# Gated DeltaNet: another order around the triangular inverse (wider squares of k and q, a new table of weight splits, z's last chunk earlier)

## The chip, the cores and the metric

The kernel runs on one core of a Trainium2 chip. Its time is the device time of that core in microseconds (us). Five engines work in parallel, each in its own fixed order: TensorE (PE in the profile; PEld is its weight load), VectorE (DVE), ScalarE (ACT), GpSimd (POOL) and SyncE (SP), which issues most transfers. An instruction that waits holds up everything behind it on its engine.

## The reference

A trunk of two layers over 256 tokens of width 1024. Each layer is half a SwiGLU, a token mixer, half a SwiGLU; the mixer of layer 0 is a gated DeltaNet with 8 heads of 128, that of layer 1 windowed attention. Only the first mixer is touched:

```python
proj = h @ w_in                       # q, k, v (1024 columns each), z (1024), b, a (8 each)
qkv = silu(causal_depthwise_conv(qkv, w_conv))          # 4 taps along time
q = l2norm(q) * 128 ** -0.5; k = l2norm(k)              # x / sqrt(sum x*x + EPS)
beta = sigmoid(b); g = -exp(A_log) * softplus(a + dt_bias)
# per head and chunk of time, g summed up along the chunk:
L   = strict_lower((k * beta) @ k.T * decay)
sol = solve((I + L), [v * beta, k * beta * exp(g)])     # unit triangular
u, w = sol
# then over the chunks: v_new = u - w S;  o = (q exp(g)) S + (q k.T * decay) v_new
#                       S = S exp(g_last) + (k exp(g_last - g)).T v_new
y = (rmsnorm(o, out_norm) * silu(z)) @ w_out
```

All is float32. A product with a weight is made of three fast products: the weight is split in a high half (`whi`) and the rest (`wlo`), and so are the activations.

## The kernel before, in words

A chunk of 256 columns of `w_in` (`wcols`) comes as two pieces of 512 KB (`raw`, four buffers). `split` casts each to `whi` on ACT (L307) and makes `wlo = raw - whi`, on DVE as one instruction (L309) or on GpSimd as four (L314); `npool` says for how many of the chunk's two pieces GpSimd does it. `whi` and `wlo` have five buffers each. The products are L360 to L362: a chunk has two halves of 24 products each (8 rows of blocks by three products, and each piece serves four of these rows).

`gdn` runs through the chunks in the order z 0 and 1, z 2, k 0 to 3, v 0 to 3, q 0 to 2, z 3, q 3. `conv` does a chunk of k, v or q: 24 products into a PSUM tile `pcv` (four such buffers), the first tap on ACT into `cv` and three taps on DVE (L924), silu on ACT. Behind a chunk, generators go on by a step at each `tick` of a ticker, so that their work mixes into the products of the next chunks:

- `kpost`: transposes a chunk of k (`pkn`), copies it twice to `kk2` (`kd` and `keg` are its halves; L726, L727), sums the squares (`sumsq`, four squares with accumulators on ACT, L718), multiplies k by itself (`pkk`), makes `br` and `nbr` on DVE (L739 to L742) and scales `kd` and `keg` on GpSimd (L744, L745).
- `blocks(g)`, after k 1 and k 3, for half the heads: cuts out the 32x32 diagonal blocks (`d32`, L762), scales them (L765) and masks them (`tri16` and `off16`, L767), all on GpSimd, and makes a power for v's scale (`ks`, L769).
- `inverse`, after k 3: inverts all 16x16 diagonal blocks on DVE (L777 to L815, 22 instructions that depend on each other), in three steps with a yield between, and adds the two generators `chain(0)` and `chain(1)`, which double the blocks to 128x128 by small products (`pt1`, `py`, `px`) with copies between.
- `vpost` and `qpost`: transposition, scale, squares and products of v and q. `state` and `first` do the recurrence; `post` and `turn` normalise the output (`so`, `fo`, `on`) and transpose it (`poT`).

The order on each engine is set when the program is compiled: a scheduler with a model of the engines' times takes the instructions that are ready, in program order where it can choose. `issue_after(ins)` ties an instruction behind another. `self.hold = [a, b, ins...]` lets a weight pieces pass and ties the casts and splits of the next ones, until b pieces are through, behind `ins`.

Of the kernel before, what the change touches and what calls it, by code (L numbers as in the profile page):

```python
# [11 lines left out]
AF = mybir.ActivationFunctionType  # L12
# [201 lines left out]
class Kern:  # L214
# [162 lines left out]
    def proj_T(self, out, w, f, nrm):  # L377
        fs = slice(f * P, (f + 1) * P)
        for k in range(KT):
            wh, wl = w(k, fs)  # L380
            self.mm3(out, wh, wl, nrm.h.hi(k), nrm.h.lo(k), k == 0, k == KT - 1)
# [296 lines left out]
    def gdn(self, nrm, prep, w_in, w_out, after):  # L678
# [43 lines left out]
        def kpost(c):  # L722
            g, hs = c // 2, slice(2 * c, 2 * c + 2)
            loc = slice(2 * (c % 2), 2 * (c % 2) + 2)
            pv = transp(lambda i: kT[:, 2 * c + i, :], "pkn")
            nc.scalar.copy(kd[:, hs, :], pv[:, 0])  # L726
            nc.scalar.copy(keg[:, hs, :], pv[:, 1])  # L727
            sumsq(pv, ssk, 2 * c)
            yield
            beta, eG, eS = res["beta"], res["eG"], res["eS"]  # L730
# [7 lines left out]
            a = ssk[:, :, hs]  # L738
            nc.vector.tensor_scalar_add(a, a, EPS)  # L739
            nc.vector.reciprocal(br[:, :, hs], a)  # L740
            nc.vector.tensor_mul(br[:, :, hs], br[:, :, hs], beta[:, :, hs])
            nc.vector.tensor_scalar_mul(nbr[:, :, hs], br[:, :, hs], -1.0)  # L742
# [10 lines left out]
        def blocks(g):  # L753
# [4 lines left out]
            us = slice(8 * g, 8 * g + 8)  # L758
            raw = self.y1([P, 8, 32], "d32")
# [6 lines left out]
            for j, m in enumerate(("tri16", "off16")):  # L766
                nc.gpsimd.tensor_tensor(out=d2[:, j, us, :], in0=raw,  # L767
                                        in1=M[m].unsqueeze(1).to_broadcast([P, 8, 32]), op=ALU.mult)
            nc.gpsimd.tensor_tensor(out=sv[:, :, gs], in0=ssk[:, :, gs],  # L769
                                    in1=self.phalf.rearrange("p (t h) -> p t h", t=NT), op=ALU.pow)  # L770

        def inverse():
# [21 lines left out]
            yield  # L794
# [13 lines left out]
            yield  # L808
# [6 lines left out]
            nc.vector.transpose(yx[:, 1].rearrange("p u c -> p (u c)"), yx[:, 0].rearrange("p u c -> p (u c)"))  # L815
            late["yx"] = yx
            tk.add(chain(0), chain(1))

        def chain(g):
# [14 lines left out]
            nc.scalar.copy(t32, blockwise(self.psB("pt1"), off, X0))  # L834
# [79 lines left out]
        def conv(col0, dst, npool, start):  # L914
            w = self.wcols(w_in, col0, npool)
            for f in range(2):
                ct = col0 // P + f
                ps = self.psA("pcv")
                self.proj_T(ps[:, :T], w, f, nrm)
                c = self.c1([P, T], "cv")  # L920
                nc.scalar.activation(c, ps[:, :T], AF.Copy, scale=wc[:, 3, ct:ct + 1])
                for j in (2, 1, 0):
                    s = 3 - j
                    nc.vector.scalar_tensor_tensor(  # L924
                        out=c[:, s:], in0=ps[:, 0:T - s], scalar=wc[:, j, ct:ct + 1],
                        in1=c[:, s:], op0=ALU.mult, op1=ALU.add)
# [11 lines left out]
        def zgate(t, hs, keep=lambda ins: ins):  # L938
            z = zs[:, t, hs]
            keep(nc.scalar.activation(z, z, AF.Silu))  # L940
            keep(nc.gpsimd.tensor_tensor(
                out=z, in0=z, in1=onb.unsqueeze(1).to_broadcast([P, hs.stop - hs.start, P]), op=ALU.mult))
# [7 lines left out]
        def then(*steps):  # L950
            for st in steps:
                r = st()
                if r is not None:
                    yield from r
                    yield
# [11 lines left out]
        def zmore(n):  # L967
            for c in range(zc[0], zc[0] + n):
                w = self.wcols(w_in, 3 * D + c * 256)
# [6 lines left out]
        for c in range(4):  # L976
# [5 lines left out]
            conv(D + c * 256, lambda f: kT[:, 2 * c + f, :], c // 2, [then(*steps)])  # L982
# [96 lines left out]
        for c in range(4):  # L1079
# [292 lines left out]
```

## Time and profile before

| what | value |
|---|---|
| median of three runs | 1023.0 us (1020.8, 1023.0, 1023.43) |
| the profiled execution | 1021.12 us |
| its span | 1019.3 us |
| its granted TensorE clock, mean | 0.995 |
| PE busy | 999.8 us, 98% |
| DVE, ACT, POOL busy | 641.8, 551.7, 242.6 us |
| the DeltaNet stage | about 195 to 372 us of the span |
| DVE in 272 to 298 us | 25.97 of 26.00 us busy |

The times of the trace count from the start of the span. A line of the trace's timeline has start, duration, engine, line, operation, output and inputs with their tile names, shapes and, in brackets, the idle time ahead of it and what ended it. A row of a grouped view has the count, the busy time, the mean of one in ns and the idle time ahead. Lines (L777 and so on) are those of the kernel before.

### The profile page before, as it was taken

To read this page: it belongs to the slowest core of one execution; us is meant where nothing else is said; L and a number is where in the kernel's file an instruction comes from. 1 tells how busy PE (TensorE), PEld (TensorE's weight loads), DVE (VectorE), ACT (ScalarE), POOL (GpSimd) and SP (SyncE) were. 2 spreads that over 40 slices of the span, in tenths; PEclk is the share of its full clock that TensorE was granted. 3 is DMA by queue.
4 is the path that set the end of the run, shared out by engine and by line. 5 is a ranking of instruction groups with operands and counts; after the bars stand their busy time and mean duration, and the time that the engine had idled before them with its cause. 6 is when DMAs were issued, how large, how long until landed. Compare 5 with 4: busy or idle time off the path is not lost.

```text
span 1019.3 us, 16506 instructions
## 1 busy us (share of the span) xinstructions
PE 999.8 (98%) x6195; PEld 871.7 (86%) x6195; DVE 641.8 (63%) x971; ACT 551.7 (54%) x1007; POOL 242.6 (24%) x311
## 2 busy tenths in 40 slices
PE   8999999999989899999999999999999999999997
PEld 7888888899979788888888888888898678888886
DVE  5866654666894666666646666664578756666544
ACT  5756544457856545555434555553367646555432
POOL 0125510017852201222200123220021402222100
PEclk9999999999999999999999999999999999999999
DMA  7766666644452336666666666676563426666661
GB/s 247 236 187 194 198 198 178 202 138 149 128 168 64 104 104 203 187 189 192 198 191 186 188 185 200 186 199 200 188 200 111 144 89 212 197 186 186 204 188 42
DMA packets 135317, 177.05 MB, mean 174 GB/s; under 512 B 7251, under 2 KB 120261, under 8 KB 135237
## 3 DMA queue, kind: packets, MB, share of 16 engines
q1 hardware_dynamic: 132032, 171.46, 55.2%
q10 hardware_dynamic: 3204, 4.53, 1.6%
q8 instruction: 49, 0.80, 0.3%
q14 instruction: 32, 0.25, 0.1%
HBM read 174.92 MB, written 1.05 MB: 173 GB/s over the span
## 4 chain that ended last, share of the span: by engine, by line
PE 63%; issue 1%; DVE 1%; DMA 1%; ACT 0%; SPq 0%; POOLq 0%; POOL 0%; ACTq 0%
PE pg L367 11%; PE pu L367 11%; PE acc L362 7%; PE acc L360 7%; PE acc L361 7%; PE pu L368 6%; PE pg L368 6%; PE pgu L362 1%; PE pgu L361 1%; PE pgu L360 1%; PE pq L360 1%; PE pq L362 1%; PE pq L361 1%; PE psc L1196 1%; PE po L1240 1%
## 5 line engine op out<-in xcount | busy, mean ns | idle before, releaser
L309 DVE TENSOR_TENSOR wlo<-raw,whi 128x1024 fp32r<-128x1024 f32 (+1 forms) x304 | 375.1, 1237 | 201.3 <-ACT whi L307 199.9
L307 ACT CAST whi<-raw 128x1024 fp32r<-128x1024 f32 (+1 forms) x318 | 330.3, 1046 | 184.1 <-PE acc L362 82.6
L367 PE MATMUL pg<-hs,whi 128*128 128x512 f32 x624 | 218.7, 392 | 0.0
L367 PE MATMUL pu<-hs,whi 128*128 128x512 f32 x624 | 218.4, 391 | 0.0
L368 PE MATMUL pu<-hs,wlo 128*128 128x256 f32 x624 | 175.1, 281 | 0.0
L368 PE MATMUL pg<-hs,wlo 128*128 128x256 f32 x624 | 174.3, 280 | 0.0
L475 POOL TENSOR_TENSOR act<-act,gate 128x256 f32<-128x256 f32 x78 | 58.5, 750 | 353.2 <-DVE act L474 338.6
L367 PEld LDWEIGHTS pg<-hs,whi 128*128 128x128 f32 x624 | 116.7, 187 | 25.7
L367 PEld LDWEIGHTS pu<-hs,whi 128*128 128x128 f32 x624 | 116.7, 187 | 25.5
L361 PE MATMUL acc<-wlo,ah 128*128 128x512 f32 (+1 forms) x340 | 128.4, 378 | 0.0
L362 PE MATMUL acc<-whi,al 128*128 128x512 f32 (+1 forms) x340 | 128.3, 377 | 0.0
L360 PE MATMUL acc<-whi,ah 128*128 128x512 f32 (+1 forms) x340 | 127.8, 378 | 0.0
L368 PEld LDWEIGHTS pg<-hs,wlo 128*128 128x128 f32 x624 | 117.9, 189 | 0.4
L368 PEld LDWEIGHTS pu<-hs,wlo 128*128 128x128 f32 x624 | 117.9, 189 | 0.0
L360 PEld LDWEIGHTS acc<-whi,ah 128*128 128x128 f32 x340 | 64.0, 188 | 12.0
L361 PEld LDWEIGHTS acc<-wlo,ah 128*128 128x128 f32 x340 | 64.0, 188 | 11.8
L362 PEld LDWEIGHTS acc<-whi,al 128*128 128x128 f32 x340 | 63.9, 188 | 11.9
L478 POOL TENSOR_SCALAR ah<-act 128x256 fp32r<-128x256 f32 x78 | 66.4, 852 | 6.7
L464 ACT COPY gate<-pg 128x256 f32<-128x256 f32 x78 | 28.8, 369 | 55.3 <-PE pg L368 55.3
L473 ACT COPY act<-pu 128x256 f32<-128x256 f32 x78 | 28.9, 370 | 53.8 <-PE pu L368 53.8
L360 PE MATMUL pcv<-hs,whi 128*128 128x256 f32 x192 | 55.1, 287 | 2.3 <-DVE cv L924 2.3
L99 POOL TENSOR_TENSOR rst<-var,mhalf 128x1 f32<-128x1 f32 x10 | 5.6, 557 | 213.8 <-DVE var L97 213.8
(340 smaller groups left out, 1584.4 us busy)
## 6 DMA issues: line engine op xcount, KB each, us to landing
raw<-in_ffn_w_gu_dram SPq DMA_DIRECT2D x156, 512.0 KB, 4.3
raw<-in_ffn_w_down_dram SPq DMA_DIRECT2D x88, 512.0 KB, 4.2
raw<-in_a_w_in_dram SPq DMA_DIRECT2D x32, 512.0 KB, 4.2
raw<-in_ffn_w_gu_dram SPq DMA_DIRECT2D x40, 256.0 KB, 4.7
raw<-in_b_w_in_dram SPq DMA_DIRECT2D x12, 512.0 KB, 4.8
raw<-in_a_w_out_dram SPq DMA_DIRECT2D x8, 512.0 KB, 3.7
raw<-in_b_w_out_dram SPq DMA_DIRECT2D x8, 512.0 KB, 3.6
nw<-in_ffn_norm_dram ACTq DMA_DIRECT2D x3, 512.0 KB, 4.1
```

The source lines that it names most:

```text
L307: nc.scalar.copy(hi[:, c], raw[:, c])
L309: nc.vector.tensor_tensor(out=lo[:, c], in0=raw[:, c], in1=hi[:, c].bitcast(F32), op=ALU.subtract)
L360: nc.tensor.matmul(out, lhsT=lh, rhs=rh, start=start, stop=False)
L361: nc.tensor.matmul(out, lhsT=lh, rhs=rl, start=False, stop=False)
L362: return nc.tensor.matmul(out, lhsT=ll, rhs=rh, start=False, stop=stop)
L367: nc.tensor.matmul(out, lhsT=lh, rhs=r2, start=start, stop=False)
L368: return nc.tensor.matmul(out[:, :T], lhsT=ll, rhs=rh, start=False, stop=stop)
L464: nc.scalar.copy(g, pg[:, T:])
L473: nc.scalar.copy(a, pu[:, T:])
L475: nc.gpsimd.tensor_tensor(out=a, in0=a, in1=gates[f], op=ALU.mult)
L478: ahead[2] = nc.gpsimd.tensor_scalar(oh, a, 1.0, None, op0=ALU.mult)
L1196: nc.tensor.matmul(out, lhsT=qT[:, j, b * P:(b + 1) * P], rhs=kz[:, kv, :, kt * P:(kt + 1) * P], start=True, stop=True)
```

## The change

- The squares of a chunk of k or q are one instruction of 512 columns on ACT, written in place in PSUM, and a sum on DVE, in place of four squares with accumulators. The two copies to `kk2` become one. `br` and `nbr` move from `kpost` to `blocks`, for four heads at once.
- The scaling of `kd` and `keg` moves to a generator `kscale`, tied on GpSimd behind the last mask (`late["d"]`); the power `ks` is tied there as well.
- `inverse` has no yields and no longer adds the chain. The three taps on DVE of v's second chunk are tied behind its end (`late["inv"]`), and so is the split of the second piece of v's third chunk.
- `chain`, `kscale`: added after v's second chunk; the chain's first products are tied behind the last products of a `conv` called so far (`late["mm"]`).
- `npool` may name the pieces. k 0 to 3: 0, 0, 1, 1 of two pieces on GpSimd becomes 0, 1, 1, 0; v 0 to 3: the second piece each becomes none, both, the first, the second; z 3: none becomes the second.
- z's chunk 3 moves from behind q's chunk 2 to behind v's chunk 0. z's gate is multiplied on GpSimd in pieces of two heads.

```diff
     def wcols(self, w, c0, npool=0):
         src = w[:, c0:c0 + 256].rearrange("(k p) f -> p k f", p=P)
+        pool = npool if isinstance(npool, tuple) else range(2 - npool, 2)
         pieces = [self.wpiece(src[:, 4 * i:4 * i + 4, :], 4, 256,
-                              eng=self.nc.gpsimd if i >= 2 - npool else None) for i in range(2)]
+                              eng=self.nc.gpsimd if i in pool else None) for i in range(2)]
...
         def sumsq(pv, ss, h0):
-            for i in range(2):
-                for t in range(NT):
-                    j = self.small([P, P], "junk", 1)
-                    nc.scalar.activation(j, pv[:, t, i, :], AF.Square, accum_out=ss[:, t, h0 + i:h0 + i + 1])
+            nc.scalar.activation(pv, pv, AF.Square)
+            nc.vector.tensor_reduce(out=ss[:, :, h0:h0 + 2], in_=pv, axis=AX.X, op=ALU.add)
...
-            nc.scalar.copy(kd[:, hs, :], pv[:, 0])
-            nc.scalar.copy(keg[:, hs, :], pv[:, 1])
+            nc.scalar.copy(kk2[:, :, hs, :], pv)
...
-            yield
-            nc.gpsimd.tensor_tensor(out=kd[:, hs, :], in0=kd[:, hs, :], in1=bc(eS, 0, hs), op=ALU.mult)
-            nc.gpsimd.tensor_tensor(out=keg[:, hs, :], in0=keg[:, hs, :], in1=bc(eG, 1, hs), op=ALU.mult)
+
+        def kscale():
+            eG, eS = res["eG"], res["eS"]
+            for c in range(4):
+                hs = slice(2 * c, 2 * c + 2)
+                with self.tc.issue_after(late["d"].ins):
+                    nc.gpsimd.tensor_tensor(out=kd[:, hs, :], in0=kd[:, hs, :], in1=bc(eS, 0, hs), op=ALU.mult)
+                    nc.gpsimd.tensor_tensor(out=keg[:, hs, :], in0=keg[:, hs, :], in1=bc(eG, 1, hs), op=ALU.mult)
+                yield
...
-                nc.gpsimd.tensor_tensor(out=d2[:, j, us, :], in0=raw,
-                                        in1=M[m].unsqueeze(1).to_broadcast([P, 8, 32]), op=ALU.mult)
-            nc.gpsimd.tensor_tensor(out=sv[:, :, gs], in0=ssk[:, :, gs],
-                                    in1=self.phalf.rearrange("p (t h) -> p t h", t=NT), op=ALU.pow)
+                late["d"] = nc.gpsimd.tensor_tensor(out=d2[:, j, us, :], in0=raw,
+                                                    in1=M[m].unsqueeze(1).to_broadcast([P, 8, 32]), op=ALU.mult)
+            with self.tc.issue_after(late["d"].ins):
+                nc.gpsimd.tensor_tensor(out=sv[:, :, gs], in0=ssk[:, :, gs],
+                                        in1=self.phalf.rearrange("p (t h) -> p t h", t=NT), op=ALU.pow)
...
-            nc.vector.transpose(yx[:, 1].rearrange("p u c -> p (u c)"), yx[:, 0].rearrange("p u c -> p (u c)"))
+            late["inv"] = nc.vector.transpose(yx[:, 1].rearrange("p u c -> p (u c)"),
+                                              yx[:, 0].rearrange("p u c -> p (u c)"))
             late["yx"] = yx
-            tk.add(chain(0), chain(1))
...
-            nc.scalar.copy(t32, blockwise(self.psB("pt1"), off, X0))
+            with self.tc.issue_after(late["mm"].ins):
+                pt = blockwise(self.psB("pt1"), off, X0)
+            nc.scalar.copy(t32, pt)
...
-        def conv(col0, dst, npool, start):
+        def conv(col0, dst, npool, start, behind=None):
...
-                for j in (2, 1, 0):
-                    s = 3 - j
-                    nc.vector.scalar_tensor_tensor(
+                with ExitStack() as later:
+                    if behind is not None:
+                        later.enter_context(self.tc.issue_after(behind.ins))
+                    for j in (2, 1, 0):
+                        s = 3 - j
+                        nc.vector.scalar_tensor_tensor(
...
-            conv(D + c * 256, lambda f: kT[:, 2 * c + f, :], c // 2, [then(*steps)])
+            conv(D + c * 256, lambda f: kT[:, 2 * c + f, :], int(c in (1, 2)), [then(*steps)])
...
         for c in range(4):
             vT = self.c2([P, 2, T], "vT")
-            conv(2 * D + c * 256, lambda f: vT[:, f, :], 1, [vpost(c, vT)])
+            if c == 2:
+                self.hold = [1, 2, late["inv"]]
+            conv(2 * D + c * 256, lambda f: vT[:, f, :], ((), (0, 1), (0,), (1,))[c], [vpost(c, vT)],
+                 late["inv"] if c == 1 else None)
+            if c == 0:
+                zmore(1)
+            if c == 1:
+                tk.add(chain(0), chain(1), kscale())
...
-            if c == 2:
-                n = 2 * zc[0]
-                w = self.wcols(w_in, 3 * D + 3 * 256)
-                for t in range(NT):
-                    zproj(3, t, w)
-                    zgate(t, slice(n, H))
-                    tk.tick()
```

The new order on the engines, at three places. First GpSimd, around the masks of the second half of the heads. Before (`wlo_3019` is the second piece of v 3, `d2` the masked blocks, `ks` the power):

```order
L769 TENSOR_TENSOR ks_1910<-ssk_1909,phalf_79 128x2x4
L314 TENSOR_TENSOR wlo_2857<-raw_2858,whi_2856 128x256 x4
L765 TENSOR_TENSOR d32_2608<-d32_2608,knbr_1912 128x256
L744 TENSOR_TENSOR kk2_1908<-kk2_1908,gexp_2116 128x256
L745 TENSOR_TENSOR kk2_1908<-kk2_1908,gexp_2116 128x256
L767 TENSOR_TENSOR d2_2607<-d32_2608,tri16_958 128x256
L767 TENSOR_TENSOR d2_2607<-d32_2608,off16_967 128x256
L314 TENSOR_TENSOR wlo_3019<-raw_3020,whi_3018 128x256 x4
L769 TENSOR_TENSOR ks_1910<-ssk_1909,phalf_79 128x2x4
L765 TENSOR_TENSOR d32_2781<-d32_2781,knbr_1912 128x256
L767 TENSOR_TENSOR d2_2607<-d32_2781,tri16_958 128x256
```

and now (`wlo_2727` is the second piece of z 3, `wlo_2798` and `wlo_2807` are both of v 1, `wlo_2879` is the first of v 2):

```order
L314 TENSOR_TENSOR wlo_2727<-raw_2728,whi_2726 128x256 x4
L314 TENSOR_TENSOR wlo_2798<-raw_2799,whi_2797 128x256 x2
L770 TENSOR_TENSOR d32_2487<-d32_2487,knbr_1912 128x256
L314 TENSOR_TENSOR wlo_2798<-raw_2799,whi_2797 128x256 x2
L772 TENSOR_TENSOR d2_2482<-d32_2487,tri16_958 128x256
L772 TENSOR_TENSOR d2_2482<-d32_2487,off16_967 128x256
L775 TENSOR_TENSOR ks_1910<-ssk_1909,phalf_79 128x2x4
L314 TENSOR_TENSOR wlo_2807<-raw_2808,whi_2806 128x256 x4
L314 TENSOR_TENSOR wlo_2879<-raw_2880,whi_2878 128x256 x4
L770 TENSOR_TENSOR d32_2647<-d32_2647,knbr_1912 128x256
L772 TENSOR_TENSOR d2_2482<-d32_2647,tri16_958 128x256
```

The scalings of `kd` and `keg` (L744, L745) are gone from ahead of the second `tri16` mask and now stand behind it; the splits of z 3, v 1 and the first piece of v 2 stand ahead of it.

Second DVE, at the inverse. Before, at its start (`cv` are the taps of v, `wlo_3379` is a piece of q):

```order
L777 STREAM_TRANSPOSE tw_2790<-d2_2607 128x512
L780 TENSOR_TENSOR inv_2792<-tw_2790 128x256
L309 TENSOR_TENSOR wlo_3379<-raw_3380,whi_3378 128x1024
L781 COPY inv_2793<-inv_2792 128x256
L924 SCALAR_TENSOR_TENSOR cv_2935<-pcv_2910,wc_1902,cv_2935 128x255
L782 MEMSET inv_2793 128x16
L790 TENSOR_TENSOR itmp_2797<-inv_2793,inv_2792 128x8
L924 SCALAR_TENSOR_TENSOR cv_2935<-pcv_2910,wc_1902,cv_2935 128x254
```

and now its end, and what stands behind it (`cv_2840` and `cv_2871` are v 1, `wlo_2888` is the second piece of v 2, `wlo_3116` the first of v 3):

```order
L817 TENSOR_TENSOR yx_2685<-tw_2656,blk16_953 128x512
L819 STREAM_TRANSPOSE yx_2685<-yx_2685 128x512
L933 SCALAR_TENSOR_TENSOR cv_2840<-pcv_2815,wc_1902,cv_2840 128x255
L933 SCALAR_TENSOR_TENSOR cv_2871<-pcv_2846,wc_1902,cv_2871 128x255
L309 TENSOR_TENSOR wlo_2888<-raw_2889,whi_2887 128x1024
L309 TENSOR_TENSOR wlo_3116<-raw_3117,whi_3115 128x1024
L309 TENSOR_TENSOR wlo_3300<-raw_3301,whi_3299 128x1024
L933 SCALAR_TENSOR_TENSOR cv_2840<-pcv_2815,wc_1902,cv_2840 128x254
L933 SCALAR_TENSOR_TENSOR cv_2871<-pcv_2846,wc_1902,cv_2871 128x254
L933 SCALAR_TENSOR_TENSOR cv_2840<-pcv_2815,wc_1902,cv_2840 128x253
```

All 22 instructions of the inverse now stand in a row, with nothing between; the taps of v 1 and the split of v 2's second piece follow it.

Third PE, in v's third chunk. Before, its second piece is `whi_2856` and `wlo_2857`, which GpSimd splits:

```order
L362 MATMUL pcv_2865<-hs_1816,wlo_2851 128x256
L360 MATMUL pcv_2865<-hs_1817,whi_2856 128x256
L361 MATMUL pcv_2865<-hs_1817,whi_2856 128x256
L362 MATMUL pcv_2865<-hs_1817,wlo_2857 128x256
L360 MATMUL pcv_2865<-hs_1817,whi_2856 128x256
```

and now, at the first product that reads `wlo_2888` (`pcv_2893` and `pcv_3005` are the two halves of v 2):

```order
L363 MATMUL pcv_3005<-hs_1816,wlo_2879 128x256
L361 MATMUL pcv_3005<-hs_1817,whi_2887 128x256
L362 MATMUL pcv_3005<-hs_1817,whi_2887 128x256
L363 MATMUL pcv_2893<-hs_1817,wlo_2888 128x256
L361 MATMUL pcv_2893<-hs_1817,whi_2887 128x256
```

All products of both halves that can do without `wlo_2888` have moved ahead of the first that reads it, and that split now comes from DVE, behind the inverse.

More of the change, by code (lines that the diff above doesn't have):

```diff
@@ L758, in blocks @@
             us = slice(8 * g, 8 * g + 8)
+            hs = slice(4 * g, 4 * g + 4)
+            a = ssk[:, :, hs]
+            nc.vector.tensor_scalar_add(a, a, EPS)
+            nc.vector.reciprocal(br[:, :, hs], a)
+            nc.vector.tensor_mul(br[:, :, hs], br[:, :, hs], res["beta"][:, :, hs])
+            nc.vector.tensor_scalar_mul(nbr[:, :, hs], br[:, :, hs], -1.0)
             raw = self.y1([P, 8, 32], "d32")
@@ L918, in conv @@
                 ps = self.psA("pcv")
[L919 removed]
+                late["mm"] = self.proj_T(ps[:, :T], w, f, nrm)
                 c = self.c1([P, T], "cv")
                 nc.scalar.activation(c, ps[:, :T], AF.Copy, scale=wc[:, 3, ct:ct + 1])
[L922 to L926 removed]
+                with ExitStack() as later:
[4 more added lines that the diff above has]
+                        nc.vector.scalar_tensor_tensor(
+                            out=c[:, s:], in0=ps[:, 0:T - s], scalar=wc[:, j, ct:ct + 1],
+                            in1=c[:, s:], op0=ALU.mult, op1=ALU.add)
                 with self.tc.issue_after(res["exp"].ins):
@@ L940, in zgate @@
             keep(nc.scalar.activation(z, z, AF.Silu))
-            keep(nc.gpsimd.tensor_tensor(
-                out=z, in0=z, in1=onb.unsqueeze(1).to_broadcast([P, hs.stop - hs.start, P]), op=ALU.mult))
+            for h in range(hs.start, hs.stop, 2):
+                z = zs[:, t, h:h + 2]
+                keep(nc.gpsimd.tensor_tensor(out=z, in0=z, in1=onb.unsqueeze(1).to_broadcast([P, 2, P]), op=ALU.mult))
         def zgates():
```

14 lines of the change are left out of this document (3 added, 11 removed).

## The prediction

> **What bounds the kernel now.** I read the page first: the busy line and the chain that ended last.
>
> ```profile
> PE 999.8 (98%) x6195; PEld 871.7 (86%) x6195; DVE 641.8 (63%) x971; ACT 551.7 (54%) x1007; POOL 242.6 (24%) x311
> PE 63%; issue 1%; DVE 1%; DMA 1%; ACT 0%; SPq 0%; POOLq 0%; POOL 0%; ACTq 0%
> ```
>
> TensorE is busy for 98% of the span, and the chain names no other engine with more than 1%. So work taken off another engine is worth only the time for which TensorE stands still or runs at a lower clock. Next I read the waits of PE in the DeltaNet stage (195 to 375 us; columns: engine, operation and line, what it waited for, us in total, times, longest) and the stage cut into windows (columns: window, its length, busy us and count of PE, PEld, DVE, ACT and POOL, granted clock, DMA share, GB/s).
>
> ```profile
> PE poT L1063 <- DVE on L1056: 3.1, 1, 3.1
> PE pcv L360 <- DVE cv L924: 2.3, 2, 1.5
> PE py L830 <- ACT t L834: 2.0, 1, 2.0
> PE pt L830 <- DVE yx L815: 0.5, 1, 0.5
> ```
>
> ```profile
> 272.00:298.00 26.00, 23.24 (x223) 22.68 (x223) 25.97 (x50) 15.78 (x29) 17.41 (x20) 1.00 0.53 163
> 298.00:322.00 24.00, 22.01 (x517) 20.53 (x503) 14.35 (x31) 15.22 (x41) 7.88 (x10) 0.93 0.34 110
> 347.00:350.80 3.80, 0.89 (x8) 0.92 (x9) 2.17 (x10) 1.96 (x12) 2.01 (x2) 1.00 1.03 350
> 350.80:354.30 3.50, 3.50 (x19) 3.21 (x17) 1.03 (x5) 1.32 (x7) 0.00 (x0) 0.52 0.12 40
> ```
>
> The stage stands still for 7.9 us in all (3.1 + 2.3 + 2.0 + 0.5). The first two windows hold the place that the change rewrites: between 272 and 298 DVE is full (25.97 of 26.00), since the triangular inverse, the convolutions and the weight splits share it, and PE still lost only 2.8 us there. The last two rows are the tail: 3.1 us of waiting, then 3.5 us at a granted clock of 0.52. At most 2.8 (272 to 298), 2.0 (298 to 322) and 0.07 x 24 = 1.7 (clock 0.93 there), 6.5 in all, can be won around the inverse.
>
> **What sets PE's time at the new order.** A product of a weight chunk passes every 0.12 us, and the last squares of k end just ahead of 255.70 (timeline of PE):
>
> ```profile
> 239.78 0.28 PE L362 MATMUL pcv<-hs,wlo 128*128 128x256 f32 x1
> 239.90 0.28 PE L360 MATMUL pcv<-hs,whi 128*128 128x256 f32 x1
> 255.70 0.36 PE L360 MATMUL pcv<-hs,whi 128*128 128x256 f32 x1
> ```
>
> In the changed order these stand between there and the first product that reads the low half split behind the inverse (wlo_2888): 4 of v's chunk 0, 48 of z's chunk 3, 48 of v's chunk 1, 14 and 14 of chunk 2, 128 x 0.12 = 15.4 us, and four transposes of v, some 0.5. PE arrives at 255.7 + 15.9 = 271.6. Nothing else may run then: the chain needs the inverse, and chunk 3 of v needs a PSUM buffer whose convolution on DVE is tied behind the inverse as well.
>
> **When the inverse starts.** It waits for the second tri mask on GpSimd. The timeline of POOL before has the prices:
>
> ```profile
> 247.44 2.83 POOL L314 TENSOR_TENSOR wlo<-raw,whi 128x256 fp32r<-128x256 f32 x4 [3.28 <-ACT whi L307]
> 256.08 1.65 POOL L769 TENSOR_TENSOR ks<-ssk,phalf 128x8 f32<-128x8 f32 x1 [1.40 <-DVE ssk L739]
> 267.38 2.65 POOL L769 TENSOR_TENSOR ks<-ssk,phalf 128x8 f32<-128x8 f32 x1
> 270.00 0.61 POOL L765 TENSOR_TENSOR d<-d,knbr 128x256 f32<-128x256 f32 x1
> 270.69 0.74 POOL L767 TENSOR_TENSOR d<-d,tri 128x256 f32<-128x256 f32 x1
> ```
>
> "Masks first" is true of kd and keg, whose eight products leave the place ahead of the masks, but the new table of splits puts four whole ones (z 3, both of v 1, the first of v 2) and a power ahead of the second mask. The first waits for a cast into the weight buffer that k's chunk 3 frees, about 247.5. From there: four splits of 2.83, two scalings of 0.61, two tri masks and one off mask of 0.74, one power of 2.15 (between 1.65 and 2.65): 11.3 + 1.2 + 2.2 + 2.2 = 16.9, so 264.4. The earliest is 261.7: the cast of v 2's first weight needs the buffer that v's chunk 0 frees with its last products, at 255.7 + 4 x 0.12 = 256.2; with 1.05 for a cast (row 345.00 below) it is done at 257.3 or a little later, then 2.83 + 0.61 + 0.74. Before, the second mask ended at 271.4: the inverse does move some 7 us forward.
>
> **How long it runs.** The groups of DVE between 271 and 298, by form (busy us and mean ns of one):
>
> ```profile
> L309 DVE TENSOR_TENSOR wlo<-raw,whi 128x1024 fp32r<-128x1024 f32 x5 | 8.4, 1679 | 0.0
> L924 DVE SCALAR_TENSOR_TENSOR cv<-pcv,wc,cv 128x255 f32<-128x255 f32 x8 | 3.7, 485 | 0.0
> ...
> L805 DVE TENSOR_TENSOR tw<-iw,inv 128x512 f32<-128x512 f32 x1 | 1.2, 1200 | 0.0
> L777 DVE STREAM_TRANSPOSE tw<-d 128x512 f32<-128x512 f32 x1 | 1.1, 1117 | 0.3 <-POOL d L767 0.3
> L812 DVE STREAM_TRANSPOSE tw<-tw 128x512 f32<-128x512 f32 x1 | 1.1, 1101 | 0.0
> L802 DVE TENSOR_TENSOR tw<-inv 128x512 f32<-128x512 f32 x1 | 1.1, 1072 | 0.0
> L790 DVE TENSOR_TENSOR itmp<-inv 128x8 f32<-128x8 f32 x2 | 1.0, 492 | 0.0
> L813 DVE TENSOR_TENSOR yx<-tw,blk 128x512 f32<-128x512 f32 x1 | 0.9, 896 | 0.0
> L781 DVE COPY inv<-inv 128x256 f32<-128x256 f32 x1 | 0.8, 830 | 0.0
> L793 DVE TENSOR_TENSOR inv<-inv,itmp 128x8 f32<-128x8 f32 x2 | 0.8, 381 | 0.0
> L807 DVE TENSOR_REDUCE inv<-tw 128x64 f32<-128x512 f32 x1 | 0.7, 732 | 0.0
> L804 DVE TENSOR_REDUCE iw<-tw 128x64 f32<-128x512 f32 x1 | 0.7, 696 | 0.0
> L815 DVE STREAM_TRANSPOSE yx<-yx 128x512 f32<-128x512 f32 x1 | 0.7, 693 | 0.0
> L780 DVE TENSOR_TENSOR inv<-tw 128x256 f32<-128x256 f32 x1 | 0.5, 495 | 0.0
> L809 DVE COPY tw<-inv 128x512 f32<-128x512 f32 x1 | 0.5, 469 | 0.0
> ```
>
> These thirteen groups of the inverse make 11.0 us, five smaller ones 2.0: 13.0. Some of it is slowed by GpSimd; elsewhere a DVE instruction grew the moment a GpSimd split began:
>
> ```profile
> 222.56 0.17 DVE L639 TENSOR_SCALAR gr<-gr 128x16 f32<-128x16 f32 x1
> 222.77 0.63 DVE L638 TENSOR_TENSOR gr<-gr,gs 128x16 f32<-128x16 f32 x1
> 222.64 2.83 POOL L314 TENSOR_TENSOR wlo<-raw,whi 128x256 fp32r<-128x256 f32 x4 [23.38 <-ACT whi L307]
> ```
>
> Undisturbed, the four 8-wide products would take 0.17 each (1.1 less), the copy at most 0.47 (0.4 less), two transposes 0.69 like the third (0.8 less), L805 1.07 like L802 (0.1 less): 10.6, with gaps between dependent instructions about 11.0. If each of the twelve products with two operands in SBUF waited 0.5 (0.63 against 0.17): 17. I take 13.5, near the trace's own 13.0, because the power, the eight kd and keg products (0.61) and one split (2.83) keep GpSimd busy under the inverse as it was in the trace (17.41 of 26.00).
>
> The Trainium skill ("SBUF — State Buffer", "Who interferes with whom") says that a DVE instruction with two SBUF inputs contends with a GpSimd instruction that reads SBUF. The row of 0.63 agrees. By that rule without exception the inverse would run its 17 us, and without it 11.0; it speaks against kd and keg placed where they now are.
>
> **The sum.** The inverse ends at 264.4 + 13.5 = 277.9. Behind it in DVE's queue come two steps of convolution (2 x 0.485) and the split wlo_2888 (1.68, the mean with GpSimd busy): PE goes on at 280.5, a stall of 280.5 - 271.6 = **+8.9** (bounds: 3.3, with 261.7, 11.0 and 1.23 for the split; 12.3, with 17).
>
> PE then has 20 products, 2.4 us, before chunk 3 of v needs the PSUM buffer of chunk 1. DVE has two more splits and three convolution steps ahead of that: 2 x 1.4 + 3 x 0.485 = 4.3, so a second wait of **+1.9** (1.5 to 2.5).
>
> After the 3.1 us wait of the tail the clock was 0.52 for 3.5 us, worth 1.7 us. The new stall is longer, but 20 products at half pace run partly into the second wait: **+0.6** (0 to 1.7). The Trainium skill ("TensorE: Matmul & The Clock Gate", Part 1) has half rate after an idle window of about 3.4 us; the row of 0.52 agrees in size, and the sum by it would be 1.7 in place of 0.6.
>
> The tail. Rows of ACT and PE:
>
> ```profile
> 345.00 1.05 ACT L307 CAST whi<-raw 128x1024 fp32r<-128x1024 f32 x1 [3.64 <-DMA raw<-in_ffn_w_gu_dram]
> 345.95 0.27 ACT L1048 ACTIVATE junk<-po 128x128 f32<-128x128 f32 x1
> 349.91 0.30 PE L1063 MATMUL poT<-ident,on 128*128 128x128 f32 x1 [3.10 <-DVE on L1056]
> ```
>
> From the first square of po to the transposition of on, 3.96 us pass. In the changed order the last transposes of q and the last products of po stand right ahead of that transposition, and on ACT one 512-wide square goes first (0.3 to 1.1 by the 0.27 of a 128-wide one, 0.6 taken). The wait becomes 4.6 where it was 3.1: **+1.5** (+1.0 to +3.0, if the cast's DMA is late as well).
>
> Gone: the two waits for cv (**-2.3**) and the one for yx (**-0.5**), because the inverse is done when its chain starts; of the wait of py **-1.3** (0 to -2.0), since the other half's 32 small products stand in front.
>
> At nothing: the squares on ACT (15.78 of 26.00 busy) and their eight new reductions on DVE (0.70 each by L804), under PE's products except as counted in the tail; br and nbr, fewer and wider, wait for GpSimd's queue anyway; z's gate in pieces, used only in the tail. If GpSimd's cover were gone, z's four last pieces would cost some 0.6 each. z's chunk 3 keeps its 48 products; its two loads on SP's queue move ahead of those of v 1 to q 2, where the DMA share of 0.34 to 0.53 leaves room.
>
> 8.9 + 1.9 + 0.6 + 1.5 - 2.3 - 0.5 - 1.3 = +8.8. The profiled run took 1021.1, three others 1020.8 to 1023.4 with a median of 1023.0; on the mean of the four, 1022.1, this is **1031**; on the profiled run itself 1029.9.
>
> **Rivals.**
> 1. Not slower (0.22): v's second chunk and z cover the inverse nearly whole. Price: stall 3.3, second wait 1.5, tail +1.0, and all 6.5 of idleness and low clock between 272 and 322 gone: -0.7, 1021.4. It decides if the inverse starts by 262 and runs 11. For it: GpSimd lost kd and keg ahead of the masks. Against: four splits stand there instead, and GpSimd reads SBUF under the inverse.
> 2. Mild (0.23): 264.4, but 11.0 long: the split ends at 264.4 + 11.0 + 1.0 + 1.2 = 277.6, stall 6.0; 6.0 + 1.9 + 1.0 - 4.1 = +4.8, 1027.
> 3. Blocked (0.15): 17 long, stall 12.3, second wait 2.5, clock 1.7, tail +3.0, less 4.1: +15.4, 1037.5.
>
> The forecast itself has 0.38, 1031 give or take 3.5; 0.02 lies elsewhere. The range is 1020 to 1038: from rival 1 less its scatter to rival 3. About 0.3%, 3 us, can be told from no change: below 1020 lies part of rival 1 and what is elsewhere, 0.12; the rest of rival 1 and the low edge of rival 2 are the same, 0.16; slower 0.72.
>
> **What would show it.** Right: a wait of PE at pcv for the split wlo of 6 to 12 us near 272 to 281, the inverse as one block on DVE between about 264 and 278, waits for cv smaller than 2.5, poT at 4 to 5, a window near clock 0.5 after the stall. Wrong: the inverse starts before 262 or ends before 275; PE finds other work there; or the loads of weights run late where I gave z's move nothing.

## The result, and the profile after

The changed kernel takes 1036.7 us (median of four runs, 1036.3 to 1037.6); the kernel before took 1023.2 in the same comparison. The ratio is 1.0139, with a 95% interval of 1.0121 to 1.0156: slower by 13.5 us. Forecast were 1031 and a range of 1020 to 1038. Executions of the same kernel differ, mostly by their granted TensorE clock: in the comparisons below the kernel before took 1019.6 us (clock 1.000) to 1029.8 us (clock 0.991), so the time of a single run says little without its trace.

First the page of the changed kernel: span and busy line.

```profile
span 1034.5 us, 16446 instructions
PE 1004.2 (97%) x6195; PEld 877.2 (85%) x6195; DVE 648.6 (63%) x970; ACT 546.5 (53%) x945; POOL 245.7 (24%) x319
```

The span of the profiled run grew by 15.2 us (1019.3 to 1034.5). TensorE has the same 6195 products and is busy 4.4 us longer, so 4.4 us went to a lower clock and 10.8 us to standing still. The waits of PE in the DeltaNet stage (195 to 390 us; us in total, times, longest) say where it stands:

```profile
PE pcv L363 <- DVE wlo L309: 7.6, 1, 7.6
PE poT L1079 <- DVE on L1072: 4.0, 1, 4.0
PE py L834 <- issue: 3.4, 1, 3.4
PE po L1016 <- DVE Dt L905: 1.9, 1, 1.9
PE pt L834 <- issue: 1.7, 1, 1.7
PE acc L361 <- ACT oT L1082: 0.5, 1, 0.5
```

The wait for wlo is the forecast one, the wait for `on` is the tail's. "issue" means that TensorE stood still and the profile shows nothing that it waited for. The two waits on "issue", 5.1 us together, have no forerunner before and were not forecast; nor was the one for `Dt` (the decay times the products of q and k). The four waits of before, two for `cv` and one each for `t` and `yx`, are gone. Next DVE at the inverse (timeline: start, duration, instruction, and in brackets the idle time ahead):

```profile
264.36 1.09 DVE L783 STREAM_TRANSPOSE tw<-d 128x512 f32<-128x512 f32 x1 [4.50 <-POOL d L772]
...
266.69 0.55 DVE L796 TENSOR_TENSOR itmp<-inv 128x8 f32<-128x8 f32 x1
...
276.33 0.71 DVE L819 STREAM_TRANSPOSE yx<-yx 128x512 f32<-128x512 f32 x1
276.96 0.83 DVE L933 SCALAR_TENSOR_TENSOR cv<-pcv,wc,cv 128x255 f32<-128x255 f32 x2
277.71 4.69 DVE L309 TENSOR_TENSOR wlo<-raw,whi 128x1024 fp32r<-128x1024 f32 x3
```

The inverse starts at 264.36, when GpSimd's masks are there, and ends at 277.04: 12.7 us in one block (24 instructions in the trace, not 22), where it used to lie between 271.46 and 297.6. Two taps and three weight splits follow. TensorE, from its timeline:

```profile
279.12 0.58 PE L363 MATMUL pcv<-hs,wlo 128*128 128x256 f32 x1 [7.61 <-DVE wlo L309]
...
286.48 1.02 PE L834 MATMUL pt<-yx,d 32*32 32x32 f32 x96
289.21 0.45 PE L834 MATMUL pt<-yx,d 32*32 32x32 f32 x32 [1.71 <-issue]
289.49 1.44 PE L834 MATMUL py<-yx,t 32*32 32x32 f32 x96
294.31 0.65 PE L834 MATMUL py<-yx,t 32*32 32x32 f32 x32 [3.39 <-issue]
```

It stopped at 279.12 - 7.61 = 271.5 and went on at 279.12 with the first split. The next 20 products took until 283.7, the end of the first window below, where the granted clock is 0.52. Then the chain's small products run and break off twice. The windows show the clock (columns as in the prediction):

```profile
279.10:283.70 4.60, 4.58 (x20) 4.36 (x21) 4.60 (x6) 1.18 (x2) 3.90 (x3) 0.52 0.56 159
290.90:294.30 3.40, 0.02 (x3) 0.00 (x0) 1.75 (x6) 0.00 (x0) 0.00 (x0) 0.50 0.30 103
294.30:298.00 3.70, 3.69 (x46) 3.63 (x47) 2.45 (x8) 0.98 (x3) 0.00 (x0) 0.50 0.02 4
298.00:301.50 3.50, 3.50 (x73) 3.27 (x73) 1.22 (x3) 2.21 (x6) 0.60 (x1) 0.63 0.00 0
364.00:367.50 3.50, 3.48 (x17) 3.50 (x18) 1.77 (x7) 0.00 (x0) 0.70 (x1) 0.50 0.01 2
```

The account, after less before, on the profiled runs: stall for the split +7.6; waits on "issue" +5.1; `Dt` and `oT` +2.4; poT 4.0 - 3.1 = +0.9; the waits of before that are gone -4.8 (2.3 + 2.0 + 0.5). Clock after: 0.48 x 4.58 + 0.50 x 3.69 + 0.37 x 3.50 + 0.50 x 3.48 = 7.1; before, (1 - 0.52) x 3.5 = 1.7 in the tail and 0.07 x 24 = 1.7 between 298 and 322; so +3.7. Together 14.9 of the 15.2 us by which the span grew.

### The profile page after: what moved, and what is told of

It is laid out like the page before. It is cut to its first block, busy times and chain, and to the rows that moved or that the text cites. A ratio compares the mean times of both kernels' runs of the same rounds, so it can differ in the third digit from the quotient of the medians.

```text
span 1034.5 us, 16446 instructions
## 1 busy us (share of the span) xinstructions
PE 1004.2 (97%) x6195; PEld 877.2 (85%) x6195; DVE 648.6 (63%) x970; ACT 546.5 (53%) x945; POOL 245.7 (24%) x319
## 4 chain that ended last, share of the span: by engine, by line
PE 61%; issue 1%; ACT 1%; DVE 1%; DMA 0%; POOLq 0%; POOL 0%; SPq 0%; ACTq 0%
PE pg L368 11%; PE pu L368 11%; PE acc L363 7%; PE acc L361 7%; PE acc L362 7%; PE pu L369 6%; PE pg L369 6%; PE pgu L363 1%; PE pgu L362 1%; PE pgu L361 1%; PE pq L361 1%; PE pq L363 1%; PE pq L362 1%; PE psc L1205 1%; PE po L1249 1%
## 5 line engine op out<-in xcount | busy, mean ns | idle before, releaser
L363 PE MATMUL pcv<-hs,wlo 128*128 128x256 f32 x192 | 57.9, 303 | 7.6 <-DVE wlo L309 7.6
L314 POOL TENSOR_TENSOR wlo<-raw,whi 128x256 fp32r<-128x256 f32 x60 | 51.1, 881 | 57.4 <-ACT whi L307 39.6
L361 PE MATMUL pcv<-hs,whi 128*128 128x256 f32 x192 | 57.8, 301 | 0.0
```

Of the source, the lines that this page charges most:

```text
L314: eng.tensor_tensor(out=l[:, i], in0=r[:, i], in1=h[:, i].bitcast(F32), op=ALU.subtract)
L361: nc.tensor.matmul(out, lhsT=lh, rhs=rh, start=start, stop=False)
L363: return nc.tensor.matmul(out, lhsT=ll, rhs=rh, start=False, stop=stop)
```

## The experiments

**e1, the tie of the split taken away.**

```diff
-            if c == 2:
-                self.hold = [1, 2, late["inv"]]
```

> The changed kernel without the line that ties the split of v's third chunk behind the inverse; the taps of v's second chunk stay tied. In its order on DVE that split and the next one stand ahead of the inverse. Theory (the tie of the split is what stops TensorE): the wait of 7.6 us for wlo is gone, and so are the half clock and most of the two waits on 'issue' that came with it; 1024 to 1029 us. Rival (the inverse as one block stops TensorE anyway, through the PSUM buffers whose taps stand behind it): a wait of 5 to 9 us at pcv for cv takes its place, 1033 to 1038 us.

Measured: 1033.3 us (median of 6 runs), ratio 1.0095 (1.0059 to 1.0131). The rival came true. The trace is that of an execution of 1036.8 us.

```profile
PE pcv L361 <- DVE cv L933: 6.2, 2, 4.6
```

The waits of PE show no wlo any more, but 6.2 us for `cv`: a PSUM buffer of v, whose taps now are late behind the inverse. So the tie of the taps is enough by itself to stop TensorE.

**e2, the tie of the taps taken away.**

```diff
-                 late["inv"] if c == 1 else None)
+                 None)
```

> The changed kernel without the tie of v's second chunk's taps behind the inverse; the split of v's third chunk stays tied. In its order six taps are woven into the inverse and the split stands behind it as before. Theory (the tie of the split): the wait for wlo stays and grows by the six taps less the two that stood between, 4 x 0.47 = some 2 us, to 9 to 10 us; 1036 to 1040 us. Rival (the taps hold TensorE through their PSUM buffers): the wait falls below 3 us, 1026 to 1031. In this order ten products of a chunk stand between pt and py of the chain: if the two 'issue' gaps of 1.7 and 3.4 us come from fetching instructions, the second gets smaller by about the 1.2 us that these products take or more; if it is a dependency on ACT's copy, it goes to nothing.

Measured: 1032.2 us (one run). Neither size is right: wlo 3.8 and `cv` 3.4, together 7.2, near the 7.6 that it was. The tie that is left is enough for a stop of seven microseconds, now in two pieces (one trace).

```profile
PE pcv L363 <- DVE wlo L309: 3.8, 1, 3.8
PE pcv L361 <- DVE cv L933: 3.4, 1, 3.4
PE py L834 <- issue: 1.6, 1, 1.6
```

Of the two gaps on "issue" one is left, at 1.6, with ten products between pt and py. It is smaller, as a late fetch has it, and not gone, as ACT's copy would have it.

**e3, both ties taken away.** Both edits at once.

> The changed kernel with neither tie (split of v's third chunk, taps of v's second chunk); everything else of the change stays. Theory (the two ties are the whole loss): no wait over 3 us between 260 and 300, 1021 to 1026 us, the tail's 4.0 left. Rival (DVE cannot give the inverse, the taps and the splits in the time that TensorE has work for, whatever their order, because the inverse starts only when GpSimd has its masks and the chain now comes earlier): the wait moves to pt for yx at the chain's start, 4 to 8 us, and the time stays at 1029 to 1035 us.

Measured: 1026.0 us, ratio 1.0024 (0.9998 to 1.0050), from 1.0139: the ties, with what follows from them, make up most of the loss. The waits of PE:

```profile
PE poT L1077 <- DVE on L1070: 4.0, 1, 4.0
PE po L1014 <- DVE Dt L905: 1.8, 1, 1.8
PE py L834 <- ACT t L840: 1.6, 1, 1.6
PE pcv L361 <- DVE cv L933: 1.4, 2, 1.1
```

No wait over 3 us is left around the inverse, and none on "issue" worth naming. With 15 taps and two splits woven into it the inverse ends at 288.3 (its last transposition starts at 287.60), 11 us later than in the changed kernel, and TensorE had products until then. The gaps on "issue" went with the ties: here ordinary products and a wait of 1.6 for `t` stand between pt and py. The tail's waits stay.

**h1, both ties away and z's chunk 3 in its old place.**

```diff
-            if c == 0:
-                zmore(1)
...
             if c == 1:
                 tk.add(then(first))
+            if c == 2:
+                n = 2 * zc[0]
+                w = self.wcols(w_in, 3 * D + 3 * 256)
+                for t in range(NT):
+                    zproj(3, t, w)
+                    zgate(t, slice(n, H))
+                    tk.tick()
```

> The changed kernel without its two ties and with z's chunk 3 back in its old place behind q's chunk 2; squares, masks, inverse, table of splits as changed. Theory (z's 48 products covered the tail's chain of squares, power and on, and the multiplication of Dt): the wait for Dt (1.8) goes, poT falls from 4.0 to 3.1, and the time falls by 2 to 4 us against the kernel with neither tie: 1020 to 1024 us. Rival (the wide squares or z's gate in pieces make the tail longer, not z's place): the two waits stay, 1024 to 1028 us. A third way: a split of q on GpSimd stands behind the eight products of kd and keg here, and TensorE waits 1 to 3 us for it.

Measured: 1023.5 us, ratio 1.0007 (0.9988 to 1.0027). The wait for `Dt` is gone and poT is at 2.8 in place of 4.0, so z's 48 products were the cover of the tail (the third way, a split on GpSimd, cost 0.2):

```profile
PE py L834 <- issue: 2.8, 1, 2.8
PE poT L1075 <- DVE on L1068: 2.8, 1, 2.8
```

The intervals of e3 and h1 overlap; that z's place costs 2 to 3 us rests on the waits rather than on the times. What remains of the change (squares, masks, inverse without yields, table of splits) is, taken together, worth nothing that can be measured: the chain's gaps on "issue" (2.8 and 0.4) and a wait of 2.2 for `cv` stand where the waits of before stood.

**b1, the kernel before with the wide squares and the single copy alone.**

```diff
-            for i in range(2):
-                for t in range(NT):
-                    j = self.small([P, P], "junk", 1)
-                    nc.scalar.activation(j, pv[:, t, i, :], AF.Square, accum_out=ss[:, t, h0 + i:h0 + i + 1])
+            nc.scalar.activation(pv, pv, AF.Square)
+            nc.vector.tensor_reduce(out=ss[:, :, h0:h0 + 2], in_=pv, axis=AX.X, op=ALU.add)
...
-            nc.scalar.copy(kd[:, hs, :], pv[:, 0])
-            nc.scalar.copy(keg[:, hs, :], pv[:, 1])
+            nc.scalar.copy(kk2[:, :, hs, :], pv)
```

> The kernel before with one part of the change alone: one wide square and one reduction for a chunk of k or q in place of four squares with accumulators, one copy in place of two; nothing else. Theory (ACT bounds nothing here, what it gains is worth nothing): 1021 to 1025 us, within 0.3% of the kernel before, the tail's wait at poT between 2.5 and 5. Rival (ACT's copies late at py and the tail's squares are on TensorE's path): 1017 to 1020 us.

Measured: 1021.4 us, ratio 0.9985 (0.9966 to 1.0004), poT 3.1. No change, as expected: ACT's time is not TensorE's here.

**c1, the kernel before with the wide squares and with kd and keg scaled behind the masks.** The edit is b1's and that of the change for `kscale` and `late["d"]` (the power `ks` is tied behind the masks too), with `tk.add(chain(0), chain(1), kscale())` at the end of the inverse.

> The kernel before with the wide squares and with kd and keg scaled behind the masks; z, ties, table of splits, inverse as before. Theory (the inverse starts 2 to 5 us earlier, and what it frees is worth the waits for cv, yx and py, 4.8 us, at most): 1017 to 1021 us. Rival (the chain's start is set by TensorE's products and DVE's load, not by the masks): no change, 1020 to 1024 us; or a wait of 1 to 3 us at pcv for a split on GpSimd that now stands behind the eight products.

Measured: 1029.6 us, ratio 1.0083 (1.0058 to 1.0108). Theory and "no change" both missed. The inverse did start earlier (268.77 in place of b1's 271.03), and the waits of PE are more, and longer:

```profile
PE poT L1067 <- DVE on L1060: 4.0, 1, 4.0
PE pt L834 <- DVE yx L819: 3.0, 1, 3.0
PE pcv L362 <- issue: 2.9, 1, 2.9
PE py L834 <- issue: 1.4, 1, 1.4
PE pcv L362 <- POOL wlo L314: 1.3, 3, 0.8
```

The split on GpSimd behind the eight products is late, as the rival said, but for 1.3 us alone. More goes to the chain, which TensorE now reaches 3.0 us before the inverse is done, to "issue" behind it, and to the tail, whose order differs too. The gap of 2.9 stands between two ordinary products, 128 pairs of weight load and product behind the one of 1.4. The trace is that of an execution of 1033.1 us, 3.4 above the median, so not all of these waits are in the median's 8 us. Moving one group of instructions on GpSimd went with another order in three other places; which of these would follow from the masks alone is open.

**k1, the changed kernel without the products that scale kd and keg.**

```diff
-                tk.add(chain(0), chain(1), kscale())
+                tk.add(chain(0), chain(1))
```

> The changed kernel with the eight products on GpSimd that scale kd and keg left out (so that part of the state is computed without its decay); everything else as in the changed kernel. It measures what GpSimd's products cost the inverse. Theory (a product with two operands in SBUF waits for a product of GpSimd): the inverse, 12.7 us from its first to its last transposition in the changed kernel, runs 10.8 to 11.6 us, the wait for wlo falls from 7.6 to 5.5 to 6.7, and the tiny products L796 and L799 stay below 0.2 us each. Rival (its instructions are as long by themselves): 12.3 us or more, the wait 7.2 to 7.8.

Measured: 1031.5 us (one run). The inverse on DVE:

```profile
263.68 1.08 DVE L783 STREAM_TRANSPOSE tw<-d 128x512 f32<-128x512 f32 x1 [4.52 <-POOL d L772]
...
265.99 0.17 DVE L796 TENSOR_TENSOR itmp<-inv 128x8 f32<-128x8 f32 x1
...
273.59 0.71 DVE L819 STREAM_TRANSPOSE yx<-yx 128x512 f32<-128x512 f32 x1
```

It runs 10.6 us (263.68 to 274.30) in place of 12.7, the second of the small products L796 takes 0.17 in place of 0.55, and the wait for wlo is 5.6 in place of 7.6. GpSimd's eight products cost 2.1 us on DVE and 2.0 on TensorE; the rest of the 5 us between the two kernels lies in the gaps on "issue" (3.9 in place of 5.1) and in the clock, and one run cannot tell what of it comes from the edit. That DVE's two-operand products wait for GpSimd's is shown by this; it agrees with the Trainium skill ("SBUF — State Buffer", "Who interferes with whom").

**g1 and g2, on the waits for "issue".** In the trace of the changed kernel the second gap lies 128 pairs of weight load and product behind the first, 256 instructions: 32 of pt and 96 of py. The transfers have a queue for instructions, q8, over the same transfer engines. TensorE's 6195 products and as many weight loads are 12390 instructions, 48.4 blocks of 256, and the page of the changed kernel counts 49 packets of 16 KB on q8; g2 below, with 256 instructions more, has 50. The view of the transfers from 291.0 to 292.5 in the changed kernel holds the packet that started at 291.91, 2.4 us before TensorE went on at 294.31 (columns: packets, MB, share of the engines; first the page, then the page of g2, then the view):

```profile
q8 instruction: 49, 0.80, 0.3%
...
q8 instruction: 50, 0.82, 0.3%
...
q8 instruction: 1, 0.02, 4.5%
```

In the traces of the changed kernel, g1, g2, h1, k1, e1, e2 and c1 each of these gaps ends 2.2 to 2.6 us after the start of such a packet, 15 gaps in all.

In g1 the loads of weights from q's first chunk, second piece, on wait for the chain's second sum:

```diff
         raw = self.wp.tile(shape, F32, tag="raw", name="raw", bufs=4)
+        if self.gate is not None:
+            self.gate[0] -= 1
+            if self.gate[0] < 0:
+                with self.tc.issue_after(self.gate[1].ins):
+                    nc.vector.memset(raw[:, 0, 0:1], 0.0)
+                self.gate = None
...
+        self.gate = [1, late["Y"]]
```

> The changed kernel with one thing more: the loads of weights from q's first chunk, second piece, on wait until the chain's second sum Y has been made on DVE (a one-column memset of the buffer, put behind it), so that no weight is moved while the chain's 256 small products run. Everything ahead is as in the changed kernel: a wait of 7 to 8 us for wlo stays. Theory F1 (the two gaps on 'issue', 1.7 and 3.4 us, are TensorE's own instructions, fetched in blocks over the same transfer engines, late behind the weights): both gaps together fall from 5.1 to under 2.5 us. Theory F2 (the fetch is late whatever else is moved, since a block of 256 instructions is used up in 1.7 us): they stay at 4 to 5.5 us. Rival D (the chain waits for ACT's copies of t or a PSUM buffer): they stay as they are and are not at a multiple of 128 products. The total says little, since the weights come later: 1034 to 1042 us.

Measured: 1034.5 us (one run). The gaps fall to 0.7 and 2.0, 2.7 together:

```profile
PE py L841 <- issue: 2.0, 1, 2.0
...
PE pt L841 <- issue: 0.7, 1, 0.7
```

So about half of the 5.1 us comes from the weights that move at the same time (DMA share 0.93 between 287 and 290 in the changed kernel and 0.32 in g1), and about half stays without them. The packets say where: after the first gap the next packet starts 2.7 us after TensorE went on in the changed kernel and 1.1 us in g1, and from its start to the end of the second gap pass 2.4 us in both. F1 and F2 each hold in part; 2.7 lies in neither's range.

g2 issues the chain's first products twice:

```diff
-                pt = blockwise(self.psB("pt1"), off, X0)
+                pt = self.psB("pt1")
+                blockwise(pt, off, X0)
+                pt = blockwise(pt, off, X0)
```

> The changed kernel with the chain's first small products issued twice (the same result, written again), 128 more pairs of weight load and product on TensorE, some 1.3 us of work. Theories F1 and F2 (instruction blocks): one gap more of 2 to 4 us, gaps on 'issue' of 7 to 10 us in all, 128 pairs apart; 1039 to 1043 us. Rival D (a dependency): the gaps stay at 5.1 us or shrink, since ACT and DVE have longer; 1036 to 1038.5 us.

Measured: 1038.7 us (one run), three gaps of 0.8, 4.1 and 1.8, 6.6 us in all:

```profile
286.65 1.02 PE L834 MATMUL pt<-yx,d 32*32 32x32 f32 x96
288.44 1.31 PE L834 MATMUL pt<-yx,d 32*32 32x32 f32 x128 [0.77 <-issue]
293.81 0.65 PE L834 MATMUL pt<-yx,d 32*32 32x32 f32 x32 [4.06 <-issue]
294.26 1.48 PE L834 MATMUL py<-yx,t 32*32 32x32 f32 x96
297.54 0.65 PE L834 MATMUL py<-yx,t 32*32 32x32 f32 x32 [1.80 <-issue]
```

One gap more, at 128 pairs again, and in the middle of one kind of product, where no copy of ACT is waited for. A dependency is ruled out: these are instructions that come late. The sum is a little under the 7 expected, and the time lies between the two ranges.

**m0 and m1, the tail.** In the kernel before, ACT waits 3.64 us for the transfer of the first weight of the next SwiGLU, in front of the squares that TensorE's poT waits for. m0 ties this one cast behind the squares of po, and holds nothing of the change:

```diff
         with ExitStack() as behind:
+            if self.first is not None:
+                behind.enter_context(self.tc.issue_after(self.first.ins))
+                self.first = None
...
         post(0, 1)
+        sq = late["sq"]
...
         after(0)
+        self.first = sq
```

(`late["sq"]` is the last square of `post`.)

> The kernel before with one tie added in the tail and nothing of the change: the cast of the first weight of the next SwiGLU, for whose transfer ACT waits 3.64 us in front of the squares of po, is tied behind these squares. Theory (the tail's wait of 3.1 us at poT and the half clock behind it hang on that cast in ACT's queue): the wait falls to 0.5 to 1.8 us, the clock stays near 1.00, and the time falls by 2 to 4 us: 1017.5 to 1020. Rival (po's last products, which wait for the multiplication of Dt on DVE, set the tail): the wait stays at 2.5 to 3.5 and the time within 1.5 us of the kernel before.

Measured: 1019.4 us (12 runs), ratio 0.9985 (0.9976 to 0.9993). It is faster than both kernels, than the one before by 1.5 to 2 us.

Of m0 first ACT, then PE, then the window of the tail:

```profile
345.10 0.28 ACT L1052 ACTIVATE junk<-po 128x128 f32<-128x128 f32 x1 [3.05 <-PE po L1004]
...
346.56 1.04 ACT L311 CAST whi<-raw 128x1024 fp32r<-128x1024 f32 x1
```

```profile
349.26 0.30 PE L1068 MATMUL poT<-ident,on 128*128 128x128 f32 x1 [1.75 <-DVE on L1061]
```

```profile
347.00:351.00 4.00, 2.25 (x19) 1.85 (x18) 2.57 (x8) 1.97 (x9) 1.76 (x2) 1.00 0.97 315
```

The first four squares now wait only for po, the cast follows them, and poT waits 1.75 in place of 3.10. After that shorter wait the clock stays at 1.00. That the shorter wait is the reason is likely and not shown: in m1 the clock stays at 1.00 behind a wait of 2.7 as well. The gain is not the tail's alone either: in this trace the clock also stays at 1.00 behind the wait of 2.0 at py, where the trace of the kernel before has 0.50 for 3.41 us, and a wait of 1.6 for `X` stands there instead.

m1 is the same tie on b1.

> The same tie in the kernel before with the wide squares and the single copy. Theory: the wait at poT falls to 0.5 to 1.8 us here too, 1016.5 to 1019.5 us, 2 to 4 us below the kernel with the wide squares alone. Rival: no change against it, 1020 to 1022 us.

Measured: 1021.3 us, ratio 0.9991 (0.9977 to 1.0006), poT 2.7. The rival came true here: po's last products came later (the first square of po starts at 346.88 in place of 345.10), so they and not the cast set the tail. The same tie is worth 1.5 to 2 us in one order of the tail and nothing in another.

## Why the prediction was right, and where it was short

- **TensorE's arrival**: 271.6 forecast, 271.5 measured. Counting the products between two points of the order and multiplying by their pace in the trace was right to 0.1 us.
- **Start of the inverse**: 264.4 forecast from ten operations in GpSimd's queue, 264.36 measured. "Masks first" was indeed not first, with four splits ahead. That it fits to the tenth is luck: the first split began at 248.15, not 247.5, and the power took 1.65, not 2.15.
- **Its length**: 13.5 forecast, 12.7 measured; bounds 11.0 and 17, the lower end measured as 10.6 in k1. GpSimd's products beside it cost 2.1 us here, not 6: only products that fall on one of GpSimd's wait (L796 took 0.55 beside one of the eight and 0.15 beside the power).
- **The stall**: +8.9 forecast, 7.6 measured: the inverse ended 0.9 earlier, the two taps took 0.3 less and the first split 0.3 less (1.41 in place of 1.68). That the tied split is what ends it is shown by e1, where the wait for it is gone; that the tie of the taps alone would stop TensorE nearly as long was in the prediction as a second wait behind the first, and e1 shows it as the first (6.2).
- **Second wait and clock**, +1.9 and +0.6: the 20 products took 4.6 us in place of 2.4, +2.2, near the sum of 2.5, but by luck. There was no second wait: the products ran at a clock of 0.52, and while they did, DVE freed the PSUM buffer. The Trainium skill ("TensorE: Matmul & The Clock Gate", Part 1), which by the prediction's own sentence gives 1.7 for the clock, was nearer than the 0.6 taken (measured 2.2). A whole idle window of 3.4 us was not needed here: waits of 2.0 and 3.1 us in the kernel before were followed by the half clock too (last section).
- **The tail**, +1.5: it cost 3.3 (poT +0.9, `Dt` +1.9, `oT` +0.5). The 3.96 us from the first square of po to the transposition came out exactly (360.05 to 364.01), and the 512-wide square that was to add 0.6 was over before po came (it started at 357.42 and took 0.58). The step left out what stands ahead of po: the multiplication of `Dt` by the last products of q and k, which waits on DVE behind a weight split. z's 48 products had covered it (h1).
- **What is gone**, -4.1: the waits for `cv` and `yx` went. The step that failed is "of the wait of py -1.3": the wait for ACT did go, and a new one of 5.1 us took its place, with a clock of 0.50 from 290.37 to 300.6, which cost the products behind it 3.1 us. The prediction put the chain's two sets of small products one behind the other and saw only that ACT would be ready; it did not ask whether TensorE's instructions would be.

On the profiled runs the four parts missed by -1.3 (stall), -0.3 (second wait and clock), +1.8 (tail) and +5.8 (the chain: 5.1 and 3.1 came, 0.7 more of the old waits went, and so did 1.7 of low clock before). Together they are +6.0 on +8.8, near the 14.9 of the account.

The stall, which is the main mechanism, was foreseen in place, cause and size. The time was met less well: 1036.7 lies outside "1031 give or take 3.5", and inside the range only because the range reached up to "blocked", whose reason did not come true (the inverse ran 12.7, not 17). That part is luck. "Not slower" failed at its own condition (264.36, not 262, and 12.7, not 11).

## What to carry to other kernels

Work that is moved forward as one block is worth only what waits for it, and costs whatever is tied behind it: count the products that TensorE can still do without these, at their pace in the trace, and compare with the block's end. Look at what the work moved away had covered where it stood before, down to the last transposition of the stage. And hundreds of tiny products in a row use up instructions faster than they come, above all while weight loads run at the same time (g1); large products between them help (e2: ten between pt and py, and 1.6 us of gaps in place of 5.1).

## What the runs showed of the hardware

- TensorE waits for its own instructions. 256 of them (128 pairs of weight load and 32x32 product) were used up in 1.3 to 1.7 us and the next came 0.4 to 4.1 us late: 1.7 and 3.4 in the changed kernel, up to 4.1 in g2, 0.4 and 2.8 in h1, and 0.7 and 2.0 in g1, where the held-back weights did not move. The Trainium skill ("Runtime: NRT & Kernel Launch", "Instruction fetch mechanics") gives the block of 256 instructions, with which the distance of the gaps agrees, and calls the fetch mostly hidden; here it was not, and the measurement decides.
- The half clock comes in steps of 3.41 us. In these traces it lasts one to four such steps (3.41 us in the kernel before, 6.83 and 10.24 in the changed one), and it need not begin behind the longest gap: in the changed kernel it began at 290.37, ahead of the gap of 3.4 us (290.92 to 294.31). What goes with it is how long TensorE was busy in the step before, counting the steps from the changes of the clock. In the 13 traces, a step at full clock in which TensorE was busy for 1.55 us or less was always followed by half clock, and one with 2.0 or more never; in between both occur (1.67 us ahead of 290.37, followed by 0.50; 1.56 in m1, followed by 1.00). So the same wait of 1.99 us at py led to 0.50 in the kernel before and to 1.00 in m0, since the steps fell otherwise (the kernel before, then m0; columns as in the prediction):

```profile
299.72:303.13 3.41, 1.54 (x130) 1.51 (x131) 3.11 (x7) 1.80 (x7) 1.54 (x2) 1.00 0.51 133
303.13:306.54 3.41, 3.41 (x18) 3.41 (x17) 3.28 (x11) 1.53 (x6) 1.24 (x2) 0.50 0.47 187
...
300.35:303.76 3.41, 2.01 (x134) 1.97 (x135) 3.10 (x8) 2.27 (x8) 1.51 (x2) 1.00 0.63 177
303.76:307.17 3.41, 2.46 (x47) 2.18 (x46) 3.28 (x10) 2.43 (x6) 0.74 (x1) 1.00 0.34 136
```
